# Cross-attention's weight splits given a set order, and a difference of the up projection queued behind the token sums

## The chip, the cores and the metric

The kernel runs on one core of a Trainium2 chip, in one launch. The core has five engines that run side by side, each through its own list of instructions in the order that the build gave it: TensorE (PE; its weight loads are listed apart as PEld) multiplies matrices into PSUM, VectorE (DVE) and ScalarE (ACT) work element by element, GpSimd (POOL) does so on SBUF, and SyncE (SP) issues most of the DMAs. The metric is the device time of one execution in microseconds (us); the smaller, the better.

## The reference

One layer of a hybrid encoder, all in float32, for 1024 tokens of width 1024. Three sublayers each add to x: a mixer (windowed attention and a two-way state-space scan, merged by gates and put through an output projection), a cross-attention into 256 memory rows, and a squared-ReLU MLP. The change touches the last two:

```python
def cross_attention(h, mem_n, w_q, w_kv, w_o):
    q = (h @ w_q).reshape(b, l, X_HEADS, X_HEAD_DIM)          # 4 heads of 128
    kv = mem_n @ w_kv                                         # k, v of the 256 memory rows
...
    s = jnp.einsum('blhd,bmhd->bhlm', q, k) * (X_HEAD_DIM ** -0.5)
    p = jax.nn.softmax(s, axis=-1)
    o = jnp.einsum('bhlm,bmhd->blhd', p, v).reshape(b, l, X_HEADS * X_HEAD_DIM)
    return o @ w_o
...
    x = x + merged @ w_out[i]
    h = rmsnorm(x, norm_cross[i])
    x = x + cross_attention(h, rmsnorm(mem, norm_mem[i]), w_xq[i], w_xkv[i], w_xo[i])
    h = rmsnorm(x, norm_ffn[i])
    x = x + jnp.square(jax.nn.relu(h @ w_up[i])) @ w_down[i]
```

## The kernel before

**How a product is made.** Every float32 operand is kept as two parts that PE can multiply: a high part (ACT copies it into a rounded type) and a low part (the rest, a subtraction on POOL or DVE). `mm3` (L79 to L90) adds three matmuls for each pair of tiles: high by high (L85), high by low (L89), low by high (L90). A weight is prepared by `wload`: `split_in` loads 128 x 1024 values into a `raw` buffer (L65, SP's queue, two buffers), ACT makes `whi` (L66), POOL makes `wlo` (L69). `whi` and `wlo` are tiles of the tag `wop`, which has six buffers, so three weights are held at a time. A tile's buffer is given out in the order of the calls, when an earlier tile's last reader is done.

**What sets the order.** The program is written with a planner. It simulates the program with times of its own and writes each engine's list: of what is ready in its simulation, it takes what stands earliest in the code. Within `merge_phase`, `up_phase` and `down_phase` PE's list is as written (`manual_schedule`); in `cross_phase` the planner orders PE too. `keep_in_program_order` (the `pin` of `wload`) puts one instruction behind whatever the code wrote last on its engine. `issue_after(ins)` puts all that a block writes on the engine of `ins` behind `ins` in that engine's list, with no wait for it to finish.

**The output projection** (end of `merge_phase`) multiplies by a seven-product scheme (`Pair.products`): sums and differences of blocks, then products in the order 1, 2, 6, 5, 7, 3, 4 (steps i = 0 to 6). `units_of(i)` gives the small steps (loads, splits, differences) that are dealt out among step i's four groups of matmuls. In step 6 the first four token blocks of x are normalised, and `norm_split` (PE transposes to a tile `nt` at L152, ACT L155, DVE L156) makes them `h2T[0]`.

**Cross-attention** (`cross_phase`). `xq_unit(h, hd, w)` makes head hd's queries of token half h: 24 matmuls into `xqp` with weight tile hd of `wxq`; ACT (L901) and DVE (L902) split the result. Called with no weight, it calls `wload` itself. First come units (0,0) to (0,3), with one token block of the second half normalised and transposed behind each; the weight of unit (0,3) is loaded, pinned, behind unit (0,1), that is, ahead of unit (0,2)'s own load in the code. Then k and v, which the first phase left in DRAM (`d_kx`, `d_vx`), are loaded and split (`split_kv`, tiles `kxh`, `kxl`, `vxh`, `vxl`; through the same two raw buffers). Then scores and softmax of one token block (`probs`: twelve matmuls to `xsp`, DVE's maximum at L915, ACT's exponential at L919, POOL's division at L923) alternate with units (1,0) to (1,3), each of which loads its weight again. Values and the output projection of the attention (`xo_units`) follow.

**The start of the MLP** (`up_phase`, class `Up`). The up projection is also made by a seven-product scheme, in transposed form, with the token sums s1 to s4 on the left. `Up.sums(i, xn)` makes them for token block i out of four: transposes (L1138), then f1 to f4 on ACT (L1152) and DVE (L1153 to L1162), each put into two parts (ACT L1146, POOL or DVE L1147). The blocks f, and the results x and c of the products, share one tag with five buffers. `Up.ahead` does products 1 and 2 early for blocks 0 to 7: `pb` and `pd` (matmuls at L1222), a copy x (ACT L1243, stored at L1244), a sum c11 (DVE L1246), its square (DVE L1226, stored at L1227). `Up.start` then sets up the generator `right`, which loads the next blocks' weights (L1176) and makes the right-hand differences t5, t6 and t7 on DVE (L1195, L1196, L1198; L1201 makes a further one from t6) and puts them into two parts (ACT L1167, POOL L1168); five puts are made at once. `Up.quad` runs a block's remaining products: 1, 2, 6, 5, 7, 3, 4 for blocks that weren't begun early. Product 6 adds to the same PSUM bank as product 1, so ACT's copy c11 (L1276) must be out first.

Of the kernel before, what the change touches and what calls it, by code (L numbers as in the profile page):

```python
# [11 lines left out]
ALU = mybir.AluOpType  # L12
# [710 lines left out]
def merge_phase(kx, ins, dr, x1_open):  # L723


    nc, tc = kx.nc, kx.tc
    V, A, G, PE = nc.vector, nc.scalar, nc.gpsimd, nc.tensor
    with tc.tile_pool(name="m3", bufs=1, reuse_waits="tile") as fp, ExitStack() as right, \
# [126 lines left out]

        def units_of(i):
            units = p.units(i, None)
            if i == 6:
                h2T.extend(act_tiles(kx))
                xns = [row("k") for _ in range(4)]  # L860
                for j in range(4):
                    norm_rows(kx, fp, kx.x1[j], xns[j], g_cross)
                units = [lambda: None] * 2
                units += [lambda j=j: norm_split(kx, xns[j], h2T, j * P) for j in range(2)]
                kx.late = lambda: [norm_split(kx, xns[j], h2T, j * P) for j in range(2, 4)]
            return units
# [6 lines left out]
def cross_phase(kx, ins, dr, h2T, g_cross):  # L873
    nc, tc = kx.nc, kx.tc
    V, A, G, PE = nc.vector, nc.scalar, nc.gpsimd, nc.tensor
    with tc.tile_pool(name="p3", bufs=1, reuse_waits="tile") as mp:
# [19 lines left out]
        def xq_unit(h, hd, w=None):  # L896
            w = w or wload(kx, ins["wxq"][hd])
            ps = kx.pp.tile([P, 512], F32, tag="p", name="xqp")
            gemm_fm(kx, ps, w, h2T[h])
            t = t4k("xq")  # L900
            A.activation(t[:, 0], ps, AF.Copy)  # L901
            V.tensor_tensor(t[:, 1], ps, t[:, 0].bitcast(F32), ALU.subtract)  # L902
            q[h][hd] = t
# [44 lines left out]
        xns = [t4f("xn") for _ in range(4)]  # L948
        for j in range(4):
            norm_rows(kx, mp, kx.x1[4 + j], xns[j], g_cross)  # L950
        w3 = None
        for i in range(4):
            xq_unit(0, i, w3 if i == 3 else None)
            if i == 1:
                w3 = wload(kx, ins["wxq"][3], pin=True)
            norm_split(kx, xns[i], h2T[1], i * P)
        kxh, kxl = split_kv(dr.kx, "kx")
        vxh, vxl = split_kv(dr.vx, "vx")
        pr = [[], []]
        for i in range(4):  # L960
            pr[0].append(probs(0, i))
            xq_unit(1, i)
        oks = [kx.mp.tile([P, 4, 2, 512], F32R, tag="kt", bufs=4, name="kt") for _ in range(2)]
        pbuf = kx.mp.tile([P, 4, 2, 512], F32R, tag="kt", bufs=4, name="kt").rearrange("p a b c -> p a (b c)")

# [37 lines left out]
def up_phase(kx, ins, dr, ok, grow, x1_low):  # L1003

    nc, tc = kx.nc, kx.tc
    with tc.tile_pool(name="p4", bufs=1, reuse_waits="tile") as mp:
# [17 lines left out]
        with tc.tile_pool(name="tp", bufs=1, side="right", reuse_waits="tile") as tp:  # L1024
            up = Up(kx, ins, dr, mp, tp, {"a11": a11, "a12": a12}, grow)
            xns = [rows(4), rows(5)]
            up.ahead((0,))
            xo_units(kx, ins, 1, ok, 0, (2, 3))
            up.sums(0, xns[0])
            xo_units(kx, ins, 1, ok, 1, (2, 3))  # L1030
            up.ahead((1,))
            up.sums(1, xns[1])
            for c in range(2, 4):
                xo_units(kx, ins, 1, ok, c, (2, 3))
            xns = [rows(6), rows(7)]
            up.ahead((2, 3))
            up.sums(2, xns[0])
            up.ahead((4, 5))
            up.sums(3, xns[1])
            up.ahead((6, 7))  # L1040
            order = [b for b in range(16) if b not in up.early] + sorted(up.early)
            up.start(order, 5)
            stage = []
            for n, b in enumerate(order):
                if n == 13:
                    us, wd = down_tiles(kx)
                    wd = wd_views(wd[0])
                    raws = []

                    def load(src):  # L1050
                        raws.append(mp.tile([P, D], F32, tag="ld", bufs=2, name="sraw"))
                        nc.sync.dma_start(raws[-1], src)

                    def u_part(j):
                        split_u(kx, None, us, j, raws.pop(0))

                    def w_part(j):
                        split_wd(kx, None, wd[2 * j:2 * j + 2], j, raws.pop(0), nc.vector)

                    loads = [lambda j=j: load(dr.u[j]) for j in range(4)]  # L1060
                    loads += [lambda j=j: load(ins["wdn"][j]) for j in range(2)]
                    splits = [lambda j=j: u_part(j) for j in range(4)] + [lambda j=j: w_part(j) for j in range(2)]
                    stage += [loads[0], loads[1]]
                    for k in range(6):
                        stage.append(splits[k])
                        if k < 4:
                            stage[-1] = lambda k=k: (splits[k](), loads[k + 2]())
                up.quad(b, stage, order[n + 1] if n < 15 else None)
            wd += wd_views(kt_tile(kx))
            for j in range(2, 4):  # L1070
                raw = mp.tile([P, D], F32, tag="ld", bufs=2, name="draw")
                split_wd(kx, ins, wd[2 * j:2 * j + 2], j, raw, nc.vector if j == 2 else nc.gpsimd)
# [38 lines left out]
class Up:  # L1111
# [15 lines left out]
    def sums(self, i, xn):  # L1127
# [31 lines left out]
        put("a22", pv[1], V)  # L1159
        put("s3", f3, G)  # L1160
        V.tensor_tensor(f4, h12, f2, ALU.subtract)
        V.tensor_tensor(f4, f4, l12, ALU.add)  # L1162
        put("s4", f4, G)

    def put(self, src):
        t = self.kx.wp.tile([P, 2, 512], F32R, tag="wop", bufs=6, name="wop")
# [490 lines left out]
```

## Time and profile before

| | before |
|---|---|
| median of 3 runs | 2435.15 us (2432.84 to 2435.18) |
| profiled execution: time, span | 2433.17 us, 2431.4 us |
| PE busy (share of the span) | 2338.6 us (96%) |
| DVE, ACT, POOL busy | 1595.3, 1135.8, 900.9 us |
| granted TensorE clock, mean over the span | 0.987 |

The profile is one execution on the chip; its own time is the span from the first to the last instruction and 1.77 us around it. A line of the timeline has the start in us from the span's start, the duration in us, the engine, the line in the code, the operation, output<-input with shapes, the count, and in brackets how long the engine had been idle and what released it. SPq is SP's queue of DMA issues. A line of the table of stretches has the stretch, its length, each engine's busy time with its count of instructions (PE, PEld, DVE, ACT, POOL), the clock granted to TensorE as a share of full speed, and the DMA engines' share and rate.

### The profile page before, as it was taken

How to read it: one execution, taken by the hardware profiler on the slowest of the kernel's cores; microseconds unless marked ns; L12 is line 12 of the kernel's file. 1: busy time of each engine (PE TensorE's matmuls, PEld its weight loads, DVE VectorE, ACT ScalarE, POOL GpSimd, SP SyncE). 2: the span in 40 equal slices, each digit the busy share in tenths (PEclk: the TensorE clock that was granted, in tenths of full speed). 3: DMA queues.
4: the chain of work that ended last, by engine and by line, in shares of the span. 5: the costliest groups of instructions: out<-in, count | busy, mean ns of one | idle time of the engine just before them, and what ended most of it. 6: DMA issues, size and time to landing. Idle time of an engine off the chain costs nothing.

```text
span 2431.4 us, 32333 instructions
## 1 busy us (share of the span) xinstructions
PE 2338.6 (96%) x11868; PEld 1939.4 (80%) x11868; DVE 1595.3 (66%) x2520; ACT 1135.8 (47%) x2406; POOL 900.9 (37%) x841
## 2 busy tenths in 40 slices
PE   7899999999999999999999999998998999999998
PEld 6688888878788787877777888876986887788887
DVE  6747566575757655356658977963666456689984
ACT  5436354453635444477765442343553333233442
POOL 4235446263544525245441014214485444200010
PEclk9999999999999999999999999998999999999999
DMA  6214132231413223111116247102243335731301
GB/s 224 81 60 129 52 113 87 72 115 57 126 57 113 76 82 96 44 52 44 46 51 233 88 157 263 66 9 87 88 153 132 109 120 161 257 150 70 130 27 70
DMA packets 150318, 252.06 MB, mean 104 GB/s; under 512 B 11280, under 2 KB 86160, under 8 KB 150160
## 3 DMA queue, kind: packets, MB, share of 16 engines
q1 hardware_dynamic: 79264, 211.19, 25.6%
q10 hardware_dynamic: 70896, 38.81, 5.6%
q8 instruction: 94, 1.54, 0.3%
q14 instruction: 64, 0.52, 0.1%
HBM read 202.51 MB, written 47.45 MB: 103 GB/s over the span
## 4 chain that ended last, share of the span: by engine, by line
PE 59%; DVE 15%; POOL 8%; ACT 7%; issue 7%; DMA 3%; SPq 0%; ACTq 0%; POOLq 0%; DVEq 0%
PE dps L1427 9%; PE mps L1427 7%; PE pb L1222 6%; PE pc L1222 3%; PE zp L89 2%; PE zp L85 2%; PE zp L90 2%; PE st L466 2%; POOL prev L481 2%; DVE cx L354 1%; POOL wlo L69 1%; PE cps L85 1%; PE cps L89 1%; PE cps L90 1%; POOL cb_t L480 1%
## 5 line engine op out<-in xcount | busy, mean ns | idle before, releaser
L69 POOL TENSOR_TENSOR wlo<-raw,whi 128x1024 fp32r<-128x1024 f32 x110 | 271.0, 2467 | 632.9 <-ACT whi L66 603.2
L1427 PE MATMUL mps<-kt 128*128 128x512 f32 x1008 | 230.3, 390 | 1.4 <-DVE kt L1379 1.4
L1378 ACT ACTIVATE kt<-row 128x512 fp32r<-128x512 f32 x264 | 144.3, 620 | 184.5 <-PE dps L1427 83.0
L1427 PE MATMUL dps<-kt 128*128 128x512 f32 x1008 | 228.6, 389 | 0.0
L85 PE MATMUL cps<-kt,whi 128*128 128x512 f32 x512 | 218.6, 427 | 8.6 <-DVE cx L354 8.6
L1427 PEld LDWEIGHTS mps<-kt 128*128 128x128 f32 x1008 | 188.8, 188 | 41.7 <-DVE kt L1379 2.6
L1427 PEld LDWEIGHTS dps<-kt 128*128 128x128 f32 x1008 | 189.2, 188 | 39.3
L66 ACT ACTIVATE whi<-raw 128x1024 fp32r<-128x1024 f32 x112 | 118.0, 1055 | 182.3 <-PE qps L89 39.7
L90 PE MATMUL cps<-kt,wlo 128*128 128x512 f32 x512 | 201.8, 394 | 0.0
L89 PE MATMUL cps<-kt,whi 128*128 128x512 f32 x512 | 201.4, 393 | 0.0
L1379 DVE TENSOR_TENSOR kt<-row,kt 128x512 fp32r<-128x512 f32 x264 | 171.7, 696 | 3.3 <-ACT kt L1378 3.2
L85 PEld LDWEIGHTS cps<-kt,whi 128*128 128x128 f32 x512 | 97.7, 191 | 35.1 <-issue 16.3
L124 POOL TENSOR_TENSOR rr<-rv,mhalf 128x1 f32<-128x1 f32 (+1 forms) x50 | 38.6, 773 | 220.4 <-DVE rv L122 217.8
L89 PEld LDWEIGHTS cps<-kt,whi 128*128 128x128 f32 x512 | 97.9, 191 | 26.6 <-issue 7.5
L1168 POOL TENSOR_TENSOR wop<-w,wop 128x512 fp32r<-128x512 f32 x64 | 86.1, 1347 | 85.9 <-ACT wop L1167 80.0
L90 PEld LDWEIGHTS cps<-kt,wlo 128*128 128x128 f32 x512 | 97.4, 190 | 21.2
L500 ACT ACTIVATE ef<-rows,ebias 128x128 f32<-128x128 f32 x256 | 83.2, 391 | 53.1 <-PE cb L515 49.6
L1222 PE MATMUL pb<-kt,wop 128*128 128x512 f32 x384 | 96.2, 399 | 10.5 <-ACT c L1276 9.4
L85 PE MATMUL gps<-kt,whi 128*128 128x512 f32 x240 | 103.2, 430 | 0.0
L501 ACT ACTIVATE eb<-rows,ebias 128x128 f32<-128x128 f32 x256 | 84.3, 392 | 35.8 <-POOL rows L492 35.8
L673 DVE CUSTOM_DVE_ANT_0 t<-sps,bias 128x384 f32<-128x384 f32 (+1 forms) x128 | 64.2, 521 | 55.7 <-PE sps L672 54.8
L684 POOL TENSOR_SCALAR t<-t,den 128x384 f32<-128x384 f32 (+1 forms) x128 | 69.5, 565 | 83.3 <-DVE den L682 62.5
(372 smaller groups left out, 6437.7 us busy)
## 6 DMA issues: line engine op xcount, KB each, us to landing
rows<-d_cs ACTq DMA_DIRECT2D x128, 256.0 KB, 3.8
raw<-in_wssd_dram SPq DMA_DIRECT2D x48, 512.0 KB, 3.7
raw<-in_wup_dram SPq DMA_DIRECT2D x40, 512.0 KB, 4.0
d_u<-c SPq DMA_DIRECT2D x64, 256.0 KB, 2.5
row<-in_wdn_dram SPq DMA_DIRECT2D x28, 512.0 KB, 6.4
row<-d_u SPq DMA_DIRECT2D x28, 512.0 KB, 6.7
x<-in_x_dram SPq DMA_DIRECT2D x16, 512.0 KB, 5.8
raw<-in_wg_dram SPq DMA_DIRECT2D x16, 512.0 KB, 3.8
```

The costliest lines, as they stand in the source:

```text
L66: steps = [nc.scalar.activation(hi, raw, AF.Copy)]
L69: steps.append((eng or nc.gpsimd).tensor_tensor(lo, raw, hi.bitcast(F32), ALU.subtract))
L85: i = mm(out, l[0], r[0], start=first, stop=False)
L89: mm(out, l[0], r[1], start=False, stop=False)
L90: mm(out, l[1], r[0], start=False, stop=last)
L500: A.activation(ef[:, h], rows[:, 0, h], AF.Exp, bias=kx.ebias[:, b, j, 0, o:o + 1])
L501: A.activation(eb[:, h], rows[:, 1, h], AF.Exp, bias=kx.ebias[:, b, j, 1, o:o + 1])
L1168: self.kx.nc.gpsimd.tensor_tensor(t[:, 1], src, t[:, 0].bitcast(F32), ALU.subtract)
L1222: self.kx.nc.tensor.matmul(ps, w[:, i, ks], act[:, k, j], start=start and k == 0 and m == 0, stop=k == 3 and m == 2, skip_group_check=True)
L1378: nc.scalar.activation(t[:, j, 0], src, AF.Copy)
L1379: nc.vector.tensor_tensor(t[:, j, 1], src, t[:, j, 0].bitcast(F32), ALU.subtract)
L1427: self.kx.nc.tensor.matmul(ps[t], lt[:, k, x, ts], rt[:, k, y], start=n in (1, 2, 5) and k == 0 and m == 0, stop=k == 3 and m == 2, skip_g ...
```

## The change

There are two parts.

In cross-attention, every weight's load and split is called one unit or more ahead of its use, in the order of use. Tiles 0, 1 and 2 of `wxq` are called for in step 4 of the output projection (ahead of step 6 with its norms); tile 3, pinned, before the first unit; the second half's tiles 0, 1 and 2 behind units (0,1), (0,2) and (0,3); its tile 3 behind unit (1,0). k is called for behind unit (0,1) and v behind unit (0,2), not behind all four.

In the up projection, `sums` returns its last DVE instruction (the second half of f4, L1162), and `up.start` runs within `issue_after` of the last block's: the first three differences t5, t6 and t7 stand behind those sums in DVE's list. What `start` writes on ACT, POOL and SP is not bound by it.

```diff
@@ merge_phase
         def units_of(i):
             units = p.units(i, None)
+            if i == 4:
+                kx.xq_w = []
+                units += [lambda m=m: kx.xq_w.append(wload(kx, ins["wxq"][m])) for m in range(3)]
             if i == 6:
@@ cross_phase
-        w3 = None
+        ws = kx.xq_w + [wload(kx, ins["wxq"][3], pin=True)]
         for i in range(4):
-            xq_unit(0, i, w3 if i == 3 else None)
+            xq_unit(0, i, ws[i])
+            if i:
+                ws.append(wload(kx, ins["wxq"][i - 1]))
             if i == 1:
-                w3 = wload(kx, ins["wxq"][3], pin=True)
+                kxh, kxl = split_kv(dr.kx, "kx")
+            if i == 2:
+                vxh, vxl = split_kv(dr.vx, "vx")
             norm_split(kx, xns[i], h2T[1], i * P)
-        kxh, kxl = split_kv(dr.kx, "kx")
-        vxh, vxl = split_kv(dr.vx, "vx")
         pr = [[], []]
         for i in range(4):
             pr[0].append(probs(0, i))
-            xq_unit(1, i)
+            xq_unit(1, i, ws[4 + i])
+            if i == 0:
+                ws.append(wload(kx, ins["wxq"][3]))
@@ up_phase
-            up.sums(3, xns[1])
+            last = up.sums(3, xns[1])
             up.ahead((6, 7))
             order = [b for b in range(16) if b not in up.early] + sorted(up.early)
-            up.start(order, 5)
+            with tc.issue_after(last.ins):
+                up.start(order, 5)
@@ Up.sums
-        V.tensor_tensor(f4, f4, l12, ALU.add)
+        last = V.tensor_tensor(f4, f4, l12, ALU.add)
         put("s4", f4, G)
+        return last
```

## The prediction

> **What bounds the kernel now.** First the page's head, then a table of stretches around the two places the change touches, then the order of instructions there, engine by engine.
>
> ```profile
> span 2431.4 us, 32333 instructions
> ...
> PE 2338.6 (96%) x11868; PEld 1939.4 (80%) x11868; DVE 1595.3 (66%) x2520; ACT 1135.8 (47%) x2406; POOL 900.9 (37%) x841
> ```
>
> TensorE (PE) is busy for 96% of the span, so what can be won cheaply is its idle time, and time in which it is busy at a lower clock. The stretches (length; busy time of PE, weight loads, DVE, ACT, POOL; granted clock; DMA):
>
> ```profile
> 1545.60:1567.00 21.40, 21.06 (x93) 17.09 (x92) 21.33 (x37) 6.79 (x13) 0.00 (x0) 1.00 0.01 5
> 1637.00:1657.00 20.00, 15.77 (x65) 12.59 (x64) 3.83 (x7) 5.01 (x9) 4.67 (x2) 0.83 0.16 52
> 1657.00:1678.10 21.10, 11.32 (x38) 8.44 (x37) 3.63 (x8) 7.81 (x15) 12.16 (x9) 0.68 0.31 100
> 1678.10:1716.00 37.90, 37.36 (x222) 32.28 (x220) 26.15 (x51) 25.66 (x76) 22.56 (x31) 1.00 0.22 70
> 1831.20:1846.00 14.80, 5.42 (x13) 4.26 (x14) 13.58 (x12) 6.71 (x13) 14.80 (x10) 0.66 0.39 119
> 1846.00:1900.00 54.00, 54.00 (x235) 43.97 (x234) 27.13 (x30) 20.06 (x35) 25.23 (x20) 1.00 0.33 115
> ```
>
> Two holes: 1637 to 1678 in cross-attention, 1831 to 1846 at the start of the up projection. In both the clock falls too (0.83, 0.68, 0.66); behind each (1678 to 1716, 1846 to 1900) PE is full at clock 1.00. So a hole made shorter moves everything behind it, and I find no later idle time that waits for anything but this work.
>
> The cross-attention hole, PE's timeline (start, duration, and in brackets the idle time before it and its releaser):
>
> ```profile
> 1629.68 1.03 PE L152 MATMUL nt<-ident,xn 128*128 128x128 f32 x8
> ...
> 1636.02 1.03 PE L152 MATMUL nt<-ident,xn 128*128 128x128 f32 x8
> 1639.73 0.50 PE L85 MATMUL xqp<-kt,whi 128*128 128x512 f32 x1 [2.68 <-ACT whi L66]
> ...
> 1642.56 0.79 PE L90 MATMUL xqp<-kt,wlo 128*128 128x512 f32 x1 [1.55 <-POOL wlo L69]
> ...
> 1661.35 0.39 PE L89 MATMUL xsp<-kxl,xq 128*128 128x256 f32 x1 [1.92 <-POOL kxl L69]
> ...
> 1667.24 0.80 PE L85 MATMUL xqp<-kt,whi 128*128 128x512 f32 x1 [3.83 <-ACT whi L66]
> ...
> 1670.76 0.80 PE L90 MATMUL xqp<-kt,wlo 128*128 128x512 f32 x1 [2.29 <-POOL wlo L69]
> ...
> 1678.12 0.28 PE L85 MATMUL xsp<-kxh,xq 128*128 128x256 f32 x1
> ...
> 1679.55 0.40 PE L85 MATMUL xqp<-kt,whi 128*128 128x512 f32 x1
> ...
> 1685.02 0.28 PE L85 MATMUL xsp<-kxh,xq 128*128 128x256 f32 x1
> ```
>
> Every wait is for a split (ACT's high part L66, POOL's low part L69) of wxq or of k. Were the data late? ACT's timeline and the SP queue say no:
>
> ```profile
> 1636.71 1.05 ACT L66 ACTIVATE whi<-raw 128x1024 fp32r<-128x1024 f32 x1
> ...
> 1638.61 1.07 ACT L66 ACTIVATE whi<-raw 128x1024 fp32r<-128x1024 f32 x1
> ...
> 1657.80 1.07 ACT L66 ACTIVATE kxh<-raw 128x1024 fp32r<-128x1024 f32 x1
> ...
> 1666.12 1.07 ACT L66 ACTIVATE whi<-raw 128x1024 fp32r<-128x1024 f32 x1
> ```
> ```profile
> 1532.85 10.57 SPq L65 DMA_DIRECT2D raw<-in_wxq_dram  x4
> 1640.23 0.33 SPq L65 DMA_DIRECT2D raw<-d_kx  x1
> ```
>
> All four wxq loads were issued by 1543.4, but only two were split there. The code says why: the pinned split of tile 3 is written ahead of tile 2's, so it holds the third of three wop pairs; tile 2 must wait for tile 0's pair. ACT splits tile 3 at 1636.71, tile 2 at 1638.61, when PE has already come to unit (0,2). k and the second half's weights are written behind all of the first half's units, and are split at 1657.80 and 1666.12 for work that PE wants at once.
>
> **Part 1, the cross-attention order.** Without holes a group of transposes and a unit take 1636.02 - 1629.68 = 6.34; a unit alone 1685.02 - 1679.55 = 5.47 (transposes 0.87); one block's scores 1679.55 - 1678.12 = 1.43. From 1636.02 PE has to do transposes and unit twice (12.68), transposes (0.87), scores (1.43) and unit (1,0) (5.47): 20.45. It took 1678.12 - 1636.02 = 42.10. If all splits are early the hole gives **21.65**, its clock loss included.
>
> Are they early? The rows that price it: two POOL splits and, beside the second and alone, the same pair of DVE operations; the landing time of a wxq load.
>
> ```profile
> 1537.75 5.31 POOL L69 TENSOR_TENSOR wlo<-raw,whi 128x1024 fp32r<-128x1024 f32 x2 [3.09 <-ACT whi L66]
> ```
> ```profile
> 1540.84 3.50 DVE L1344 TENSOR_TENSOR acc<-acc 128x512 f32<-128x512 f32 x2
> ...
> 1545.70 1.42 DVE L1344 TENSOR_TENSOR acc<-acc 128x512 f32<-128x512 f32 x2
> ```
> ```profile
> raw<-in_wxq_dram SPq DMA_DIRECT2D x8, 512.0 KB, 4.1
> ```
>
> I price a load at 4.1, ACT's split at 1.07, POOL's at 2.65. Tile 3 gets its pair when unit (0,0) ends at 1629.68, so it is split by 1633.4; unit (0,3) wants it at 1636.02 + 6.34 + 0.87 = 1643.2. k's raw buffer is then free: load, ACT and POOL to 1641.6, or 1644.2 behind another split; scores want it at 1636.02 + 12.68 + 0.87 = 1649.6. That is the least slack, 5.4. Each later tile goes through one of two raw buffers at 7.8 a turn: wxq 0 by 1640, wxq 1 by 1648, wxq 2 by 1656, against needs at about 1651, 1658 and 1665. Splits of v and wxq 3 are wanted later still. The pinned split of tile 3 now waits on ACT for unit (0,0)'s end; behind it there stand only that unit's copy and the transposes' copies, which PE wants in unit (1,0) and in the scores. POOL does seven splits (18.6) in some 30 us. Moved DMAs: six SP issues, each 0.33, with nothing else on that queue between 1543 and 1640. So no stall is left that I can see, and the waits at 1623 stay as they are.
>
> The price: tile 2's split now falls into the end of the output projection's first products, near 1545, where DVE is busy 21.33 of 21.40 and PE runs behind it. Beside POOL's split the pair of L1344 took 3.50, alone 1.42: one POOL split costs DVE 2.1. If tile 2 is split after 1567 it costs nothing. I take 2.1. The Trainium skill (SBUF — State Buffer, section "SBUF: two separate sides") speaks against the change here: a DVE operation with two SBUF inputs and a reading GpSimd operation lock each other out for a whole instruction. By that rule the loss is up to the split's 2.65 and the sum 0.55 higher; the row's 2.1 agrees in kind.
>
> Part 1: 21.65 - 2.1 = **19.55**.
>
> **Part 2, the difference queued behind the sums.** DVE, SP, ACT, POOL and PE there:
>
> ```profile
> 1826.00 0.69 DVE L1195 TENSOR_TENSOR w<-raw 128x512 f32<-128x512 f32 x1 [6.82 <-DMA raw<-in_wup_dram]
> ...
> 1829.14 0.68 DVE L1153 TENSOR_TENSOR f<-kt,nt 128x512 f32<-128x512 f32 x1
> ...
> 1834.13 1.74 DVE L1201 TENSOR_TENSOR w<-raw,w 128x512 f32<-128x512 f32 x1 [1.16 <-POOL wop L1168]
> 1835.79 1.75 DVE L1162 TENSOR_TENSOR f<-f,kt 128x512 f32<-128x512 f32 x1
> ```
> ```profile
> 1821.63 0.33 SPq L1176 DMA_DIRECT2D raw<-in_wup_dram  x1
> 1822.06 0.38 SPq L1227 DMA_DIRECT2D d_u<-c  x1
> ```
> ```profile
> 1839.93 0.60 ACT L1276 ACTIVATE c<-pb 128x512 f32<-128x512 f32 x1 [0.21 <-POOL s L1147]
> ```
> ```profile
> 1832.39 1.71 POOL L1168 TENSOR_TENSOR wop<-w,wop 128x512 fp32r<-128x512 f32 x1
> ```
> ```profile
> 1840.58 5.49 PE L1222 MATMUL pb<-kt,wop 128*128 128x512 f32 x12 [9.41 <-ACT c L1276]
> 1845.86 3.13 PE L1222 MATMUL pc<-s,wop 128*128 128x512 f32 x12
> ```
> ```profile
> raw<-in_wup_dram SPq DMA_DIRECT2D x9, 512.0 KB, 4.3
> d_u<-c SPq DMA_DIRECT2D x7, 256.0 KB, 2.1
> ```
>
> L1195, the first difference, sat at DVE's head from 1819.2 to 1826.0 for a load issued at 1821.63, with the last block's sums (L1153 to L1162) behind it; L1201, which waits for POOL, came between those too. The sums' low part (L1147) frees the buffer for L1276, on which PE waited 9.41.
>
> With the order turned, L1153 needs a buffer of five: the store at 1822.06 lands at 1824.2 (I read the buffer's turn from the code; if another is free, sooner). The chain to L1162's end took 8.4, of which L1201 and its wait 2.8: 5.6, so it ends at 1829.8, not 1837.5. Queued behind it now are L1195, L1196 and L1198; for them wait the puts on ACT and POOL and PE's products 6, 5 and 7. Product 6 needs two of them: at L1195's 0.69 or, beside POOL, L1201's 1.74 each, done at 1831.2 to 1833.3, say 1832.5. The put takes 0.7 on ACT (L1276's 0.60 and a hand-over) and 1.71 on POOL; PE can start two matmuls (0.46) before the low part ends, which the third reads: 1834.4. Gain 1840.58 - 1834.4 = **6.2**, and 3.2 of the gap stays. Bounds: with no gap and full clock 9.41 + 2.55 (twelve matmuls took 5.28 to the next product; at 5.47/24 each they take 2.73), so 12; at worst L1153 stays at 1829.14, the differences run at 1.74 and a c11 pair goes first: 3 lost. I keep the slow product in the sum: in the first hole gaps of 2.68 and 1.55 with two matmuls between were enough for clock 0.83.
>
> **Sum.** 2433.17 (the profiled execution: span 2431.4 and 1.77 around it) - 19.55 - 6.2 = 2407.4. The median of the runs is 2435.15, 1.98 above; so **2409.4**. A measurement tells about 0.2%, 4.9 us, from no change.
>
> **Rivals.**
> - *The gap in part 2 closes so far that the clock stays up*: for it, the store may not gate L1153. Between 6.2 + 2.55 and 12: 2403.6 to 2406.8. The Trainium skill (TensorE: Matmul & The Clock Gate, "What's actually happening") closes the gate only after an idle window of about 3.4 us, so a gap of 3.2 might not; the 2.68 and 1.55 above speak against reading it sharply. Chance 0.14.
> - *Part 2 gives nothing*: a new wait, product 6 for its own put instead of for L1276. The c11 pairs of blocks 6 and 7 are written ahead of the differences and may be queued ahead. 2409.4 + 6.2 = 2415.6. Chance 0.13.
> - *One stall stays in cross-attention*: the planner leaves k's split behind late work on ACT or POOL. 1657.0 to 1678.1 then stays: 21.1 less scores and unit (6.9), 14.2 back: 2423.6. Against it: k is now written two units earlier, with 5.4 of slack. Chance 0.10.
> - *The change doesn't do what it says*: the planner issues the same order. 2435. It is against the code, which removes the pair taken out of turn. Chance 0.03.
> - *Slower*: the planner lays out the other engines' queues of the up projection anew, and a quad's weight load lands behind a store on SP, as stores stood behind the load at 1821.63. Each such quad shows 4.3 landing, 0.6 ACT and 1.71 POOL, 6.6. It decides from five of sixteen quads (30.7 / 6.6); six give 2435.15 - 25.8 + 39.6 = 2449. Against it: 54.00 busy of 54.00 behind 1846. Chance 0.05.
>
> The forecast keeps 0.55. Its own range is 2404 to 2415; to hold 8 in 10 I go from 2402 (part 2 in full) to 2424 (one stall left). Faster: 0.55 + 0.14 + 0.13 + 0.10 = 0.92; same 0.03; slower 0.05.
>
> **What would show it.** ACT splits wxq 2 before 1600 and k within 12 us of unit (0,1); PE's waits for L66 and L69 in cross-attention vanish, with clock 1.00 there; DVE's L1153 starts before L1195; the wait for L1276 shrinks from 9.41 to about 3, its releaser perhaps L1168. Wrong if DVE's loss near 1545 is many microseconds, if waits for whi, kxh or wlo reappear, or if new gaps stand between 1846 and the end.

## The result, and the profile after

| | before | after |
|---|---|---|
| median, first comparison | 2435.16 us (2432.84 to 2436.32, 4 runs) | 2416.94 us (2414.15 to 2417.88, 4 runs) |
| ratio, 95% interval | | 0.9924 [0.9907, 0.9942] |
| median, compared again (c_again below) | 2434.45 us (2432.08 to 2436.02, 7 runs) | 2411.15 us (2408.89 to 2412.26, 4 runs) |
| ratio, 95% interval | | 0.9903 [0.9888, 0.9918] |
| profiled execution (first comparison): time, span | 2433.17, 2431.4 us | 2414.15, 2412.4 us |

The change makes the kernel faster: 18.2 us in the first comparison and 23.3 in the second, where 25.8 was forecast. Both medians lie in the forecast's range of 2402 to 2424; the first lies above the narrower one, 2404 to 2415, that the forecast gave for its own case. After the first 860 lines the changed file's line numbers are 3 to 9 higher: L901 is now L904, L1153 L1161, L1195 L1204, L1222 L1231, L1276 L1285.

The page's head, and the table of stretches around the two places (length; busy time of PE, weight loads, DVE, ACT, POOL; granted clock; DMA), of the kernel after:

```profile
span 2412.4 us, 32332 instructions
...
PE 2332.4 (97%) x11868; PEld 1936.0 (80%) x11868; DVE 1601.5 (66%) x2520; ACT 1136.3 (47%) x2406; POOL 904.2 (37%) x841
```
```profile
1545.60:1567.00 21.40, 21.40 (x96) 17.70 (x96) 21.33 (x32) 7.04 (x13) 2.84 (x1) 1.00 0.11 38
1637.00:1657.00 20.00, 18.23 (x98) 15.33 (x98) 7.78 (x13) 9.57 (x14) 11.94 (x5) 1.00 0.47 155
1657.00:1678.10 21.10, 21.10 (x111) 18.08 (x110) 10.14 (x20) 10.45 (x30) 12.09 (x15) 1.00 0.24 76
1811.50:1827.00 15.50, 9.10 (x31) 7.03 (x31) 13.51 (x14) 7.03 (x13) 11.38 (x9) 0.78 0.41 144
1827.00:1880.00 53.00, 53.00 (x231) 43.14 (x230) 27.58 (x31) 19.29 (x35) 26.84 (x20) 1.00 0.35 121
```

The first hole is all but gone: 98 and 111 matmuls where there had been 65 and 38, at clock 1.00 where there had been 0.83 and 0.68. Missing are 1.77 us. The second hole is smaller but still there (PE 9.10 of 15.50, clock 0.78), 20 us earlier, and behind it PE is full. POOL's 2.84 in the first row is tile 2's split, where it had been 0.00.

What is left in cross-attention, on PE's and then ACT's timeline (start, duration, idle time before it and releaser), and the load on SP's queue:

```profile
1654.96 0.39 PE L85 MATMUL xsp<-kxh,xq 128*128 128x256 f32 x1 [1.55 <-ACT xq L904]
1655.69 0.38 PE L90 MATMUL xsp<-kxh,xq 128*128 128x256 f32 x1 [0.22 <-DVE xq L905]
```
```profile
1640.10 1.05 ACT L66 ACTIVATE kxh<-raw 128x1024 fp32r<-128x1024 f32 x1
...
1653.37 1.06 ACT L66 ACTIVATE whi<-raw 128x1024 fp32r<-128x1024 f32 x1 [2.36 <-DMA raw<-in_wxq_dram]
1654.33 0.58 ACT L904 ACTIVATE xq<-xqp 128x512 fp32r<-128x512 f32 x1
```
```profile
1649.65 3.21 SPq L65 DMA_DIRECT2D raw<-in_wxq_dram  x2
```

Between 1637 and 1678 PE waits for no split any more, and k is split at 1640.10, not 1657.80. But one split makes another instruction late: the second half's tile 2 (loaded from 1649.65, wanted only by unit (1,2)) stands in ACT's list ahead of unit (0,3)'s copy L904. ACT sat idle for 2.36 us until the load landed, then split, then copied; the scores need the copy.

The up projection: DVE, SP's queue, the DMA's landing times between 1800 and 1815, ACT and PE:

```profile
1805.58 0.69 DVE L1161 TENSOR_TENSOR f<-kt,nt 128x512 f32<-128x512 f32 x1
...
1806.78 1.65 DVE L1164 TENSOR_TENSOR f<-f,kt 128x512 f32<-128x512 f32 x1
1812.13 0.69 DVE L1165 TENSOR_TENSOR f<-nt,f 128x512 f32<-128x512 f32 x1 [3.70 <-DMA d_u<-c]
...
1815.93 0.67 DVE L1204 TENSOR_TENSOR w<-raw 128x512 f32<-128x512 f32 x1
...
1817.13 1.15 DVE L1205 TENSOR_TENSOR w<-raw,w 128x512 f32<-128x512 f32 x1
```
```profile
1806.65 0.33 SPq L1185 DMA_DIRECT2D raw<-in_wup_dram  x1
1807.07 0.38 SPq L1236 DMA_DIRECT2D d_u<-c  x1
...
1808.02 0.45 SPq L1185 DMA_DIRECT2D raw<-in_wup_dram  x1
```
```profile
raw<-in_wup_dram SPq DMA_DIRECT2D x2, 512.0 KB, 5.3
...
d_u<-c SPq DMA_DIRECT2D x2, 256.0 KB, 5.5
```
```profile
1820.37 0.61 ACT L1176 ACTIVATE wop<-raw 128x512 fp32r<-128x512 f32 x1
1820.89 0.58 ACT L1285 ACTIVATE c<-pb 128x512 f32<-128x512 f32 x1
```
```profile
1821.52 4.95 PE L1231 MATMUL pb<-kt,wop 128*128 128x512 f32 x12 [6.40 <-ACT c L1285]
1826.31 2.94 PE L1231 MATMUL pc<-s,wop 128*128 128x512 f32 x12
```

The order is the one meant: sums (L1161 to L1170) ahead of differences (L1204, L1205). But the sums stop in the middle: L1165 (f2, an instruction that the prediction doesn't speak of) waits 3.70 us for a store to leave its buffer. It is the store issued at 1807.07: it landed 4.96 us later, at 1812.03, with two weight loads of 512 KB under way beside it; the two stores of c in this stretch took 5.5 in the median. PE's wait shrank from 9.41 to 6.40, not to 3.2, and product 6 is still slow (4.79 to the next one).

**Where the time went, stretch by stretch.** PE's matmuls are the same 11868 in every kernel here, so the n-th matmul of one trace can be set against the n-th of another. The table gives, for each profiled execution, by how much a stretch (its ends by the times of the kernel before) became longer or shorter; a row adds up to the difference of the spans. It holds the runs of the next section too. In cross-attention the planner orders PE, and between 1640 and 1680 up to 48 of the matmuls stand in another place than in the kernel before. At 1675.6 this puts 0.2 us too much into the cross-attention column of the five rows whose next column has +0.17 to +0.20, and 0.5 too much into that of e4_pin; the next column gives it back. At 1679.55, where the orders agree again, the gain in cross-attention is 19.32 in the kernel after, 19.45 in c_again, 18.62 in e3_tile2, 20.31 in e4_pin, 17.92 in e5_c8, and 21.65 to 21.67 in the last five rows.

```
run          to 1546.1  to 1622.6  cross-attn  to 1779.8  up proj.   to the   span less
                                   to 1675.6              to 2040.1  end      2431.4
after          +2.72      -0.12     -19.50      +0.20     -2.99      +0.68    -19.02
c_again        -0.25      +0.22     -19.63      +0.19     -4.40      -0.44    -24.31
e1_part1       +1.76      +0.32     -19.56      +0.18     -0.16      -0.01    -17.47
e2_part2       +0.22      -0.68      -0.00      +0.03     -3.53      -0.60     -4.56
e3_tile2       +3.63      -0.69     -18.80      +0.18     -3.72      +0.35    -19.05
e4_pin         +2.40      +0.07     -20.81      +0.56     -3.31      -0.65    -21.74
e5_c8          -1.04      +2.06     -18.10      +0.17     -6.94      +0.92    -22.94
e6_pinlate     +2.74      +2.07     -21.63      +0.04     -4.46      +0.00    -21.24
e8_best        +2.02      +0.45     -21.63      +0.02     -3.81      -0.34    -23.29
e9_pin_c8      +2.11      +0.60     -21.64      -0.01     -6.10      +1.12    -23.91
e10_w4         +2.15      +0.53     -21.62      +0.02     -5.60      -0.28    -24.79
e11_w4c8       +1.70      -0.65     -21.62      +0.01     -5.52      -0.17    -26.26
```

The first column is a stretch that ends where the change begins. It differs by up to 4.7 us from one execution to the next; between the kernel after and c_again, which are the same program, by 3.0. That, 1.4 in the up projection and 1.1 at the end are the difference between the two profiled executions of the change. What makes the first column differ is open. The two medians of this one program differ by 5.8 us (2416.94 and 2411.15), and their ranges do not overlap. So a part of the change is read from its own column, and a median that differs by 2 us from another, or by 5 from one of another session, says little.

### The profile page after: what moved, and what is told of

It is laid out like the page before. It is cut to its first block, busy times and chain, and to the rows that moved or that the text cites. A ratio compares the mean times of both kernels' runs of the same rounds, so it can differ in the third digit from the quotient of the medians.

```text
span 2412.4 us, 32332 instructions
## 1 busy us (share of the span) xinstructions
PE 2332.4 (97%) x11868; PEld 1936.0 (80%) x11868; DVE 1601.5 (66%) x2520; ACT 1136.3 (47%) x2406; POOL 904.2 (37%) x841
## 4 chain that ended last, share of the span: by engine, by line
PE 62%; DVE 16%; POOL 7%; ACT 6%; issue 5%; DMA 4%; SPq 0%; ACTq 0%; POOLq 0%; DVEq 0%
PE dps L1436 9%; PE mps L1436 8%; PE pb L1231 6%; PE pc L1231 3%; PE zp L89 3%; PE zp L85 3%; PE zp L90 2%; PE st L466 2%; PE cps L85 2%; PE cps L89 2%; PE cps L90 2%; POOL prev L481 2%; DVE cx L354 1%; POOL cb_t L480 1%; PE dps L85 1%
## 5 line engine op out<-in xcount | busy, mean ns | idle before, releaser
L1231 PE MATMUL pb<-kt,wop 128*128 128x512 f32 x384 | 95.7, 398 | 8.1 <-ACT c L1285 6.4
```

What stands on the lines that cost most here:

```text
L1231: self.kx.nc.tensor.matmul(ps, w[:, i, ks], act[:, k, j], start=start and k == 0 and m == 0, stop=k == 3 and m == 2, skip_group_check=True)
```

## The experiments

The kernel before gave 2434.45, 2434.32 and 2434.19 in the three sessions: beside c_again, e3, e4 and e5; beside e1, e2, e6 and e8; and beside e9, e10 and e11.

**The change again (c_again).**

> The changed kernel once more, for a second trace and for the comparisons of this group. If the 2.6 us by which its first trace ran late between 419 and 956 us (ahead of everything the change touches, with the same order on every engine) is chance, that offset comes out different here; if it is a cost of the new program (its layout in memory), it is 2 to 3 us again. Time 2414 to 2418.

Measured: 2411.15 us (0.9903 [0.9888, 0.9918]). It shows the 1.43 and 0.22 us of wait in the scores (1.55 and 0.22 in the first trace) and 5.37 ahead of product 6 (6.40). Both failings are the program's, not chance. The 2.72 us that the first trace lost ahead of the change are chance: here that column is -0.25. The time lies below the expected 2414 to 2418.

**Tile 2 of the first half asked for later (e3_tile2).** This is to take the price off DVE at 1545.

```diff
-                units += [lambda m=m: kx.xq_w.append(wload(kx, ins["wxq"][m])) for m in range(3)]
+                units += [lambda m=m: kx.xq_w.append(wload(kx, ins["wxq"][m])) for m in range(2)]
...
-        ws = kx.xq_w + [wload(kx, ins["wxq"][3], pin=True)]
+        ws = kx.xq_w + [wload(kx, ins["wxq"][m], pin=True) for m in (2, 3)]
```

> The changed kernel, but tile 2 of wxq is called for, pinned, at the start of cross-attention and not in the output projection, so that its split falls near 1632 and not at 1546. Theory (the split costs DVE 2.1 us at 1546, and PE has to wait for DVE at 1567 unless it is late itself): the pair of row-sized differences there takes 1.4 us and not 3.50, and the time is 0 to 2 us below the changed kernel's. Rival (DVE has slack there and nothing is paid): DVE is quicker there, and the time is the same within 0.7 us.

Measured: 2412.9 us (0.9911 [0.9894, 0.9928]), and it can't be told from c_again. Tile 2's split is gone from there (POOL's next one is at 1633.1). But the splits of tiles 0 and 1, in unchanged places of their lists, came later, since the first load was issued at 1537.14 (1533.37 in the kernel after) and both landed later, and so POOL and DVE met near 1545 all the same, on the timelines of POOL and DVE:

```profile
1542.76 5.29 POOL L69 TENSOR_TENSOR wlo<-raw,whi 128x1024 fp32r<-128x1024 f32 x2 [6.61 <-ACT whi L66]
```
```profile
1545.82 3.50 DVE L1353 TENSOR_TENSOR acc<-acc 128x512 f32<-128x512 f32 x2
```

This is one pair at 3.50, as in the kernel before (1540.84 in the prediction's rows); the kernel after has two, at 1541.38 and 1546.23. The second column gives -0.69 here, and -0.12 and +0.22 with the split in its place. Neither theory's 1.4 for this pair came true, and a difference of 0.6 to 0.9 in single executions leaves the price open; the spread of that column (below) bounds it.

**The late split pinned where it is written (e4_pin).**

```diff
-                ws.append(wload(kx, ins["wxq"][i - 1]))
+                ws.append(wload(kx, ins["wxq"][i - 1], pin=i == 3))
```

> The changed kernel, with the second half's tile 2 pinned, so that on ACT its split stands behind the copy of unit (0,3) and no longer ahead of it. Theory (PE's waits of 1.55 and 0.22 in the first block's scores come from that split, which sits on ACT until its load has landed, with the copy behind it): both waits go, 1.5 to 2.5 us below the changed kernel. Rival (the scores' next step, softmax or the other half's transposes, is then as late): a new wait of the same size a few us later, and the same time.

Measured: 2410.16 us (0.9899 [0.9884, 0.9914]). Unit (0,3)'s copy is now ahead of the split, and the wait for it is gone. The next thing on ACT is late in its place, the copies kt of the last transposes (ACT, then PE):

```profile
1653.12 1.06 ACT L66 ACTIVATE whi<-raw 128x1024 fp32r<-128x1024 f32 x1 [1.17 <-DMA raw<-in_wxq_dram]
1654.08 1.07 ACT L155 ACTIVATE kt<-nt 128x512 fp32r<-128x512 f32 x2
```
```profile
1654.71 0.50 PE L85 MATMUL xqp<-kt,whi 128*128 128x512 f32 x1 [1.09 <-ACT kt L155]
```

Cross-attention gives 20.81, against 19.50 and 19.63 (20.31 against 19.32 and 19.45 at 1679.55): some 0.9 of the stall went, and 1.3 came back a little later, as the rival had it.

**The same split behind those copies too (e6_pinlate).**

```diff
-            if i:
+            if i in (1, 2):
                 ws.append(wload(kx, ins["wxq"][i - 1]))
...
-        pr = [[], []]
+        pr, _ = [[], []], ws.append(wload(kx, ins["wxq"][2], pin=True))
```

> The change, with one call moved: the second half's tile 2 is asked for, in a fixed place, behind the last token tile's transposed copies, where the change asks for it ahead of them and the planner puts ScalarE's split ahead of unit (0,3)'s copy. Theory A (that split, whose load lands late, is what keeps the copy and so PE back): PE's waits of 1.1 to 1.6 us and 0.2 us near 1655 are gone and nothing of 0.5 us or more takes their place between 1640 and 1676; cross-attention's part is worth 21 to 22 us, near the 21.65 of the prediction, and the time 2409 to 2410. Theory B (the copy is late by itself, or the next list position becomes late as the copies kt did with the pinned call ahead of them): a wait of 1 us or more stays between 1640 and 1676, and the part is worth 18 to 20.8 us as in the four runs of the whole change and its variants.

Measured: 2410.24 us (0.9894 [0.988, 0.9907]). ACT's list is now copy, copies, split, and the table of stretches has PE full at clock 1.00:

```profile
1653.69 0.60 ACT L904 ACTIVATE xq<-xqp 128x512 fp32r<-128x512 f32 x1 [0.78 <-PE xqp L90]
1654.19 1.08 ACT L155 ACTIVATE kt<-nt 128x512 fp32r<-128x512 f32 x2
1655.42 1.06 ACT L66 ACTIVATE whi<-raw 128x1024 fp32r<-128x1024 f32 x1
```
```profile
1640.00:1676.00 36.00, 36.00 (x193) 30.91 (x192) 18.27 (x29) 19.64 (x43) 21.66 (x18) 1.00 0.37 125
```

The stretch is worth 21.63, and 21.62 to 21.64 in the four later runs with this edit; theory A. The 2 us that the change left there are that one place in ACT's list. The median does not show them beside c_again: this profiled execution had 2.74 and 2.07 more in the two stretches ahead.

**Eight buffers of the tag c, not five (e5_c8).** No list changes; only the wait for the store goes.

```diff
-        return self.tp.tile([P, 512], F32, tag="c", bufs=5, name=name)
+        return self.tp.tile([P, 512], F32, tag="c", bufs=8, name=name)
```

> The changed kernel, with eight buffers for f, x and c in the up projection and not five; the order of every engine's list is the same, only waits for buffers differ. Theory (the last block's sums now wait 3.70 on DVE for a buffer that a store of c must leave, and that store lands 5 us after its issue): DVE runs the sums through, PE's gap ahead of product 6 shrinks from 6.4 to 2.5 to 3.5, and the time falls by 3 to 6 us, the more if the clock stays at 1.00 behind so short a gap. Rival (the differences and their puts on POOL are the next bound, and the sums' lead is lost there): the gap stays above 5 and the time within 1 us.

Measured: 2410.29 us (0.9905 [0.9891, 0.992]). f2 runs without a wait, the up projection's column is 6.94 where it was 2.99 and 4.40, and PE's wait is 3.97. What holds product 6 now (ACT, then PE):

```profile
1816.03 0.63 ACT L1176 ACTIVATE wop<-w 128x512 fp32r<-128x512 f32 x1 [1.80 <-DVE w L1207]
...
1817.09 0.58 ACT L1285 ACTIVATE c<-pb 128x512 f32<-128x512 f32 x1
```
```profile
1817.71 4.60 PE L1231 MATMUL pb<-kt,wop 128*128 128x512 f32 x12 [3.97 <-ACT c L1285]
```

The copy L1285 stands on ACT behind the put of t7, which waits for DVE's L1207. So the store's wait is real, but taking it away does not bring the forecast's 3.2. The median is not 3 to 6 us under c_again's, as was expected. The profiled execution lost 2.06 ahead of cross-attention and 1.5 more in it than c_again: behind the same two waits in the scores (1.39 and 0.22 here) the clock fell, where it stayed at 1.00 in the kernel after and in c_again (the table's row in this run):

```profile
1652.00:1660.00 8.00, 6.55 (x23) 5.32 (x24) 3.46 (x8) 4.08 (x12) 3.68 (x4) 0.79 0.32 108
```

**Each part alone (e1_part1, e2_part2).** The first is the change without `issue_after`; the second has `issue_after` alone.

```diff
-            with tc.issue_after(last.ins):
-                up.start(order, 5)
+            up.start(order, 5)
```

> The cross-attention part alone; the up projection's first difference keeps its place ahead of the last token block's sums. Theory A (each part is worth what the traces of the whole change show at its own place, and the parts add): PE is 18 to 21 us earlier at 1676 than in the kernel before, nothing more is won after it, the wait ahead of product 6 is again 9 to 10 us, and the time is 18 to 21 us under the kernel before, near 2415.5. Theory B (the parts are not independent: a PE that comes 20 us earlier to the last token block makes the up projection's wait longer): PE is again 18 to 21 us earlier at 1676 but the wait ahead of product 6 is over 11 us, and the time is 16 us or less under the kernel before, 2419 or more.

> The up projection's part alone; cross-attention as in the kernel before. Theory A (the store that VectorE's second difference f2 waits for lands late because two weight loads share the DMA with it, so that the part is worth 3.3 to 4.4 us wherever it stands): cross-attention's waits as before, f2 waits 3 to 5 us for that store, a wait of 5.5 to 6.5 us stays ahead of product 6, and the time is 3.3 to 4.4 us under the kernel before, near 2431.3. Theory B (the size of the prediction, 6.2 us, holds where cross-attention isn't changed, and what was lost in the whole change came from the earlier PE): a wait of about 3.2 us stays, and the time is about 6 us under the kernel before, near 2429.2.

Measured: 2416.8 us (0.9927 [0.9914, 0.9939]) and 2430.99 us (0.9983 [0.9974, 0.9992]). PE's wait ahead of product 6, in the first and in the second; then DVE's f2 (L1158 there) in the second:

```profile
1824.29 4.49 PE L1230 MATMUL pb<-kt,wop 128*128 128x512 f32 x12 [9.42 <-ACT c L1284]
```
```profile
1836.60 5.49 PE L1224 MATMUL pb<-kt,wop 128*128 128x512 f32 x12 [5.88 <-ACT c L1278]
```
```profile
1827.20 0.69 DVE L1158 TENSOR_TENSOR f<-nt,f 128x512 f32<-128x512 f32 x1 [3.30 <-DMA d_u<-c]
```

Theory A in both by the traces: 9.42 and 5.88 us of wait, 3.30 for the store also where cross-attention isn't changed. The first part's time is 17.5 under the kernel before, a little short of theory A's 18 to 21. The parts add as far as this can tell: by medians 17.5 + 3.3 = 20.8, half-way between the whole change's 18.2 and 23.3; by their columns 19.56 + 3.53 = 23.1, where the whole change has 22.5 and 24.0.

**The copy ahead of t7's put, with both mended places (e8_best).** The late split behind the copies, eight buffers, and:

```diff
-                up.start(order, 5)
+                up.start(order, 4)
...
-                up.quad(b, stage, order[n + 1] if n < 15 else None)
+                up.quad(b, stage, order[n + 1] if n < 15 else None), up.more() if n == 0 else None
...
-            A.activation(c11, pb, AF.Copy)
-            after()
+            copy = A.activation(c11, pb, AF.Copy)
+            with kx.tc.issue_after(copy.ins) if len(self.ready) == 3 else contextlib.nullcontext():
+                after()
```

> The run with the call moved, and two edits in the up projection: eight buffers of tag c instead of five, so that no sum waits for a store, and ScalarE's copy of the first product ahead of its split of the third difference t7, behind which the copy stood while VectorE and GpSimd still worked towards t7. Theory A (with the store's wait gone, that place in ScalarE's list is what holds product 6, and next in line is GpSimd's low half of t6, which ended 0.8 us before product 6 began in the run with eight buffers): product 6 starts 0.5 to 1.5 us earlier there, a wait of 2.5 to 3.5 us stays ahead of it or inside its first matmuls, the part is worth 7 to 8.5 us and the time is 2406 to 2408, under every other run. Theory B (the copy's place costs nothing, since the weights of product 6 are late by themselves): the wait ahead of product 6 and its first matmuls stays at 4 us or more together, and the time is that of the run with the call moved less 2.5 us.

Measured: 2409.13 us (0.989 [0.9877, 0.9904]): neither theory's time. PE's timeline, two rows of stretches, and DVE:

```profile
1813.62 0.73 PE L1232 MATMUL pb<-kt,wop 128*128 128x512 f32 x2 [1.16 <-ACT c L1286]
1815.97 2.57 PE L1232 MATMUL pb<-kt,wop 128*128 128x512 f32 x10 [1.62 <-POOL wop L1178]
1818.38 2.95 PE L1232 MATMUL pc<-s,wop 128*128 128x512 f32 x12
...
1829.79 4.38 PE L1232 MATMUL pb<-a,wop 128*128 128x512 f32 x12 [2.85 <-DVE c L1302]
```
```profile
1812.00:1824.00 12.00, 9.22 (x40) 6.85 (x39) 10.80 (x8) 6.11 (x12) 12.00 (x9) 1.00 0.40 144
1824.00:1830.00 6.00, 3.15 (x14) 2.25 (x13) 4.76 (x6) 1.27 (x2) 6.00 (x4) 1.00 0.17 65
```
```profile
1827.40 1.74 DVE L1211 TENSOR_TENSOR w<-raw,w 128x512 f32<-128x512 f32 x1 [1.17 <-POOL wop L1178]
1829.06 0.67 DVE L1302 TENSOR_TENSOR c<-c,pb 128x512 f32<-128x512 f32 x1
```

Product 6 starts early, its wait is down to 1.16 + 1.62, and its ten later matmuls run at full speed (2.41 to the next product). Eleven microseconds later 2.85 us are lost, and then product 4 runs slowly: PE now comes early to a sum, L1302, that stands on DVE behind L1211, which waits for POOL. POOL is busy without a break (12.00 of 12.00, 6.00 of 6.00). The gain was real and was given back: 3.81 in the column, less than the eight buffers alone give.

**Without the copy's move (e9_pin_c8)**, that is, the late split behind the copies and eight buffers:

> The moved call and the eight buffers of tag c together, with ScalarE's list in the up projection as the change has it. Theory A (the run that also put the copy first gave its 3 us back: a wait of 2.85 us ahead of product 4, for a sum on VectorE that stood behind a difference which waited 1.17 us for GpSimd, and a low clock behind it): here no such wait comes ahead of product 4, the up projection's part is worth 6 to 7 us as with the eight buffers alone, cross-attention's 21 to 22 us, and the time is 2405.5 to 2407.5, 2 to 3 us under the run with the copy first. Theory B (with PE arriving 2 us earlier than in the run with eight buffers alone, GpSimd, which is busy without a break from 1800 to 1823, is late in any order): the part is worth 3.5 to 5 us and the time is 2408 to 2410.

Measured: 2408.33 us (0.9895 [0.988, 0.9909]). The wait ahead of product 6 is 3.99, none comes ahead of product 4, cross-attention gives 21.64 and the up projection 6.10: theory A by the traces. The time is 0.8 us above its range and would fit theory B's, with 2.11 more ahead of the change in the profiled execution. Against the run that differs from it by the eight buffers alone (e6_pinlate), the up projection gains 1.6.

**A fourth buffer for the weights' differences (e10_w4, e11_w4c8)**, in the run with the copy moved and in the one without:

```diff
-            t5, t6, t7 = (self.tp.tile([P, 512], F32, tag="w", bufs=3, name="w") for _ in range(3))
+            t5, t6, t7, t8 = (self.tp.tile([P, 512], F32, tag="w", bufs=4, name="w") for _ in range(4))
...
-            V.tensor_tensor(t6, b21, t6, ALU.subtract)
+            V.tensor_tensor(t8, b21, t6, ALU.subtract)
             yield self.put(b22)
-            yield self.put(t6)
+            yield self.put(t8)
```

> The run with the copy first, and a buffer of its own for the fourth difference of the weights (tag w with four buffers instead of three, where the difference was written over the third one and waited until GpSimd had read that). Theory A (the wait of 1.17 us on VectorE, behind which stood the sum that product 4 waited for, was all of it): the 2.85 us ahead of product 4 shrink to under 1 us, the up projection's part is worth 7 to 8.5 us and the time is 2405 to 2407. Theory B (GpSimd's own list is the bound, busy without a break from 1800 to 1830 in that run): the wait moves to a split of GpSimd's or of ScalarE's behind it, 2 to 4 us stay between 1816 and 1832, and the time is 2408 to 2410.

> The moved call, eight buffers of tag c and four of tag w, with ScalarE's list as the planner makes it (the copy behind the split of t7). Theory A (VectorE's wait for GpSimd also delays t7 and with it the split that the copy stands behind): product 6 starts up to 1 us earlier than with eight buffers alone, and the time is 2405 to 2407. Theory B (that wait comes after t7 in VectorE's list and delays nothing that product 6 needs): as the run with the moved call and the eight buffers, within 1 us.

Measured: 2406.4 us (0.9885 [0.9868, 0.9901]) and 2406.85 us (0.9891 [0.9877, 0.9906]). In the first the wait ahead of product 4 shrinks from 2.85 to 1.87 and still ends with L1302, which now stands behind another difference on DVE; the column gives 5.60, between the theories (DVE in the last row):

```profile
1815.48 4.05 PE L1232 MATMUL pb<-kt,wop 128*128 128x512 f32 x10 [1.63 <-POOL wop L1178]
1819.37 2.94 PE L1232 MATMUL pc<-s,wop 128*128 128x512 f32 x12
...
1829.77 3.05 PE L1232 MATMUL pb<-a,wop 128*128 128x512 f32 x12 [1.87 <-DVE c L1302]
```
```profile
1827.36 1.76 DVE L1205 TENSOR_TENSOR w<-raw 128x512 f32<-128x512 f32 x1
```

Here DVE is the one that is full (5.93 of 6.00 between 1824 and 1830): while POOL works without a break each of these differences takes 1.76 where one that began with POOL idle took 0.68 (L1207 in the kernel after, 1818.80). In the second the wait ahead of product 6 is 4.15 and the column 5.52, as theory B has it: that wait came behind t7. (Its time, 1.5 under the run without the fourth buffer, would fit theory A; its wait ahead of product 6 doesn't.) The two medians are the lowest of all, 4 to 5 us under c_again's by comparisons of different sessions, but the columns say that little of it is in the up projection: the copies ahead of the late split account for 2.0, the eight buffers for 1.1 to 2.5.

## Why the prediction was right, and where it wasn't

**What bounds the kernel: right.** The holes were of PE, and all that was won in them arrived at the end (the last stretch changes by 1.2 at most).

**The dense time of cross-attention, 20.45, and the gain of 21.65: right as a size.** It is reached to 0.03 us once no stall is left (21.62 to 21.64 in five runs).

**"So no stall is left that I can see": wrong.** The step worked out when each split is ready against when PE wants *that* weight, and by this the second half's tile 2 had slack (1656 against 1665; ACT had split it by 1654.4). What it left out is who stands behind each split on ACT. It did name what is queued behind tile 3's pinned split, and not behind the others, whose places the planner chooses. A split with 10 us of slack, placed ahead of a copy with none, cost 1.55 + 0.22 us of wait. Against the rows without the stall that is 2.0 to 2.3 us in the three traces where the clock stayed up (after, c_again, e1_part1), and 3.0 and 3.7 in two others, with a wait of 2.25 (e3_tile2) and with the clock at 0.79 (e5_c8).

**Tile 2's price of 2.1 near 1545: there on DVE in some executions, mostly not in the time.** DVE and POOL of the kernel after, then DVE of c_again:

```profile
1546.23 3.50 DVE L1353 TENSOR_TENSOR acc<-acc 128x512 f32<-128x512 f32 x2
```
```profile
1546.35 2.84 POOL L69 TENSOR_TENSOR wlo<-raw,whi 128x1024 fp32r<-128x1024 f32 x1 [2.75 <-ACT whi L66]
```

```profile
1543.48 1.42 DVE L1353 TENSOR_TENSOR acc<-acc 128x512 f32<-128x512 f32 x2
```

In the first the pair took 3.50 where it took 1.42 in the kernel before, as forecast. In c_again, the same program, the split began at 1545.20, behind the pair, and the pair took 1.42. The stretch to 1622.6 is longer by -0.12 in the kernel after, and in the other ten executions with this part by -0.69 to +0.60 in eight and +2.06 and +2.07 in two (it is -0.68 without this part, in e2_part2). Both of these have two pairs at 3.50, and so have three others that lost 0.60 at most. What decides whether it reaches PE is open: PE came 1.04 early in one of the two and 2.74 late in the other. The section of the Trainium skill that the prediction weighed (SBUF — State Buffer, "SBUF: two separate sides") is borne out on DVE, as the first two rows show; whether it costs time is a matter of the path.

**The order on DVE: right; the store in the chain to L1162's end: wrong twice.** "The store at 1822.06 lands at 1824.2": the prediction took 2.1 us for it, a median over 1795 to 1850. In the kernel before this very store took 4.6 (DMA landing times there, between 1822.0 and 1822.1):

```profile
d_u<-c SPq DMA_DIRECT2D x1, 256.0 KB, 4.6
```

So the change did not slow it; its landing was mis-priced. And the buffer was not the one of L1153, which began at once, but that of f2, the fourth instruction of the sums on DVE. The two errors work against each other, so that it is partly luck how near the end of the sums came. Counted from the moment at which PE runs out of work (1831.17 in the kernel before), the prediction has that end at -1.4; it came at +0.3 in the kernel after and at -0.8 in c_again.

**From the sums' end to product 6: too short.** The prediction has 4.6 us there (1829.8 to 1834.4), for two differences and the put of the second. The kernel after and c_again both took 6.1: ACT's copy L1285, for which product 6 waits, stands behind the put of the third difference, t7. With eight buffers the sums end at -4.6, yet a wait of 3.97 stays (3.99 and 4.15 in the two later runs); with the copy ahead of that put (e8_best) it is 1.16 and 1.62, 1.2 less together. So "3.2 of the gap stays" was too little: 6.40 and 5.37 stayed, of which 1.7 and 0.6 more than forecast by the sums' later end and 1.5 by what follows it. How much of the 1.5 is the copy's place was not measured with five buffers.

**The effect of part 2.** 6.2 forecast, 3.0 to 4.5 measured in six runs, 5.5 to 6.9 in the three where eight buffers take the wait away and ACT's order is the planner's.

**The slow product: right in the kernel after** (4.79 for twelve matmuls, clock 0.78).

**The sum and the rivals.** 25.8 forecast; by the columns of the two traces it is 19.5 + 3.0 to 4.4 = 22.5 to 24.0. Of the two medians, 23.3 lies inside this and 18.2 lies 4.3 below it, in a session whose profiled execution was 2.72 late ahead of the change. That cross-attention gave 19.3 to 19.6, where 19.55 was forecast for part 1, is luck: a price of 2.1 that these two executions did not pay and a stall of 2.0 to 2.3 that was not foreseen cancel. None of the rivals came true. "One stall stays" was of the right kind, but the stall came by ACT's list, not k's, and cost 2.0 to 3.7, not 14.2. In the run with the copy moved the clock did stay up in product 6, as the first rival had it, and the time did not follow.

## What to carry to other kernels

When a piece of work is moved ahead, ask for each of its instructions not only whether it is ready in time for its own reader, but who stands behind it on its engine while it waits for its data; an early request with a late load is a wait for others. Price a DMA's landing by what is under way beside it at that moment, not by a median, and count the buffers of a ring up to the instruction that really needs the stored one. Judge a part by the stretch it touches, matched instruction by instruction, where executions differ elsewhere by more than the part is worth.

## What the runs showed of the hardware

- **The slow product does not follow the wait's length.** From the start of product 6 to the next product, 12 matmuls, took 5.28 us behind 9.41 of wait in the kernel before and 4.32 behind 9.42 in that with the first part alone, 4.79 behind 6.40, 5.28 behind 5.88, 5.29 behind 5.37 and 4.44 behind 3.97, against some 2.8 at full clock. Two waits of 1.16 and 1.62 left ten matmuls at full speed (2.41), two of 1.08 and 1.63 did not (3.89). The Trainium skill (TensorE: Matmul & The Clock Gate, "What's actually happening") has a window of about 3.4 us that runs freely, so that it matters where in it the idle time falls; a spread at the same wait agrees with that. Its rule would not have closed the gate behind 2.85 us of wait (product 4 above, 4.38), unless idle time before it counts, which no run here shows. Nor would it have behind the waits of 1.39 and 0.22 in the scores of e5_c8 (clock 0.79 from 1652 to 1660), which were as long in c_again (1.43 and 0.22) and left the clock at 1.00 there.
- **A 256 KB store landed 2.0 us after its issue, or 4.6 to 6.1 beside a 512 KB load issued within 1 us ahead of it.** On SP's queue in the kernel after, the stores issued at 1800.06 and 1814.49 took 2.0, those at 1807.07, 1807.50 and 1808.55 took 5.0, 5.2 and 6.1, with loads issued at 1806.65 and 1808.02. In the kernel before it was 2.0 at 1815.48 and 4.6 at 1822.06, with a load issued at 1821.63. That the load is the reason is argued from this order in time; no run took the load away.
